# Down projection with 20 of 22 k-tiles in seven products, weight sums from two loads, a GpSimd addition and three adding transfers

## The chip, the cores and the metric

The kernel runs on one core of a Trainium2 chip. The time is that of one execution on the device in microseconds (us). The engines are called as the profile calls them: PE is TensorE, DVE VectorE, ACT ScalarE, POOL GpSimd, and SP issues transfers. The kernel before has a median of 830.14 us over 3 runs (827.84 to 832.91).

## What is computed

One encoder block for 512 tokens of width 1024, in float32:

```python
h = rms_norm(x, norm1_pre)
q, k, v, z, xbc, dt_raw, gates = split_cols(h @ w_in, IN_SPLITS)
attn_out = gqa_attention(q, k, v) @ w_attn_proj       # after RMS norm and axial RoPE
ssd_out = ssd_branch(z, xbc, dt_raw, ...) @ w_ssd_proj
g_attn, g_ssd = split(sigmoid(gates), 2)
x = x + rms_norm((g_attn * attn_out + g_ssd * ssd_out) @ w_out, norm1_post)
h2 = rms_norm(x, norm2_pre)
gate, up = split(h2 @ w_gate_up, 2)                   # 1024 -> 2 x 2816
ffn = (silu(gate) * up) @ w_down                      # 2816 -> 1024
x = x + rms_norm(ffn, norm2_post)
```

## The kernel before

**Split products.** Every float32 product is made of three matmuls on pieces: each operand is cast to fp32r (the high part), the rest is the low part, and lo x hi, hi x lo and hi x hi are summed in PSUM. TensorE does little else than these for the whole kernel; its order is written out by hand, while a scheduler orders the other engines by when it thinks their operands are ready, and all of them work through their queues in order.

**Projection weights.** `weights()` (L103) lists the weights of the front with a letter for how the low part comes about, and `presplit()` (L136) does it. ACT casts the high part in any case (L144). With "v" DVE subtracts, with "g" POOL (L149). With "d" ACT writes the negative of the raw weights (L146), and an accumulating transfer, issued by POOL, loads the weights a second time and adds them (L147). A tile has up to 128x1024 elements; the first kv pieces have 128x864. hT is the transposed normalised input: h by DVE (L294), its high part by ACT (L183), its low part by DVE (L184).

**Down projection.** `act` holds 22 tiles of 128 k-rows x 512 tokens. `down_start()` (L1139) does the first two k-tiles while the last of the FFN still runs; `down()` (L1153) adds four more plainly, each with 24 matmuls of 128x512. The other 16 k-tiles, as pairs from two halves of k, go through a product of 2x2 blocks in seven products in place of eight (48 matmuls each). Its weight sums are formed in the tiles ch and p3 (profile name p): a block is loaded by SP, and others are added by accumulating transfers which POOL issues: `after` (L1225) and `third_weights` (L1281). A weight tile is split by `wsplit` (ACT L1195, DVE L1196), an activation tile by `asplit` into "as" (ACT L1201, DVE L1202). DVE also forms activation sums (L1312 to L1318), with both operands in SBUF, and adds finished banks to the results c (L1245). `begin` and `finish` do the last norm for a token tile t: square sums on ACT, the gain multiplications on DVE (L1257, L1264), then c * r + x (L1270) and the store. They stand between the matmuls of product 7, whose last 24 matmuls are those of the second token tile alone (by_token).

```python
stages.extend((lambda g=g: prep(g), lambda g=g: work(g)) for g in range(NG2))
...
for i, (_, work) in enumerate(stages):
    if i + 1 < len(stages):
        stages[i + 1][0]()
    work()
last(3)
```

The operands of a group are thus recorded one group ahead of its matmuls. The tiles whi and wlo have 4 buffers, "as" has 10; the pool of down() lies where a pool of the FFN was.

Of the kernel before, what the change touches and what calls it, by code (L numbers as in the profile page):

```python
# [14 lines left out]
ALU = mybir.AluOpType  # L15
# [4 lines left out]
P = 128  # L20
# [21 lines left out]
R_DTB, R_AL, R_D, R_QK, R_END = 0, 32, 64, 80, 336  # L42


PAIRS = 8
NPLAIN = 3


# [12 lines left out]
class Block:  # L61
# [41 lines left out]
    def weights(self):  # L103

        a = self.a
        for k0, kn in ((0, 3), (3, 3), (6, 2)):
            yield a["w_kv"][:, k0 : k0 + kn, :], kn * 288, "v" if k0 == 0 else "d"
        for j in range(12):
            yield a["w_xbc"][j], 1024, "g" if j < 3 else "d"
        for n in range(2):  # L110
            for i in range(4):
                yield a["w_z"][n, i], 1024, "gd"[n]
        for j in range(2 * KD):
            yield a["w_g"][j], 1024, "d"
# [1038 lines left out]
    def down(self, pool):  # L1153


        V, A, G, T = self.V, self.A, self.G, self.T
        n0, wd, act = NF - 2 * PAIRS, self.a["w_dn"], self.act
        NG2 = PAIRS // 2
        new = lambda tag, shape, bufs, dt=F32: pool.tile([P] + shape, dt, tag=tag, name=self.nm(tag), bufs=bufs)
        chain = [new("ch", [2, 512], NG2) for _ in range(NG2)]  # L1160
        p3 = [new("p3", [2, 512], NG2) for _ in range(NG2)]
        r1 = [new("r1", [256], PAIRS) for _ in range(PAIRS)]
        splits = [new("as", [2, 256], 10, F32R) for _ in range(10)]
        cs = [new("c", [512], 8) for _ in range(8)]
# [6 lines left out]
        mm3, plain, bank = self.mm3f, self.plain, self.bank  # L1171

        for k in range(1, n0):
            if k > 1:
                self.down_operands(k, pool)
                if k < n0 - 2:
                    for t, n in bank:
                        plain(k, t, n)
            if k == 1:
                gain = [new("gn", [512], 2) for _ in range(2)]  # L1180
                for i in range(2):
                    self.load(gain[i], self.a["norm2_post"][i * 512 : i * 512 + 512].partition_broadcast(P))
            if k >= 2 and k - 2 < NG2:
                self.load(chain[k - 2], blk(k - 2, 0, 0))
        for t, n in reversed(bank):
            for k in (n0 - 2, n0 - 1):
                plain(k, t, n)
# [28 lines left out]
        def product(dst, b, a, start, after=None, sums=None, by_token=None, then=None):  # L1216

            kept = []

            def prep(g):  # L1220
                w = wsplit(b(g))
                for i in range(2):
                    kept.append((asplit(a(2 * g + i)), [y[:, i * 512 : i * 512 + 512] for y in w]))
                if after:
                    G.dma_start(chain[g], after(g), accum_op=ALU.add)  # L1225

            def work(g):
                for k in (2 * g, 2 * g + 1):
                    x, wi = kept[k]
                    for t in range(1 if by_token else 2):  # L1230
                        mm3(dst[t], [y[:, t * P : t * P + P] for y in x], wi, start and k == 0)
                    if sums:
                        sums(k)
                if g == NG2 - 1:
                    if by_token:
                        by_token()
                        for x, wi in kept:
                            mm3(dst[1], [y[:, P : 2 * P] for y in x], wi)
                    if then:
                        then()  # L1240

            stages.extend((lambda g=g: prep(g), lambda g=g: work(g)) for g in range(NG2))

        def add(t, n, p, op=ALU.add):
            V.tensor_tensor(c[t, n], c[t, n], p, op)  # L1245

        half = {}

        def begin(t):

            x = [new("x2", [512], 4) if t < 2 else self.slot("a", [512], name="x2") for _ in range(2)]
# [3 lines left out]
            self.square_sum(ss[:, 0:1], c[t, 1], self.rstd[:, t : t + 1])  # L1255
            V.tensor_scalar(ss[:, 0:1], ss[:, 0:1], 1.0 / D, EPS, ALU.mult, ALU.add)
            V.tensor_tensor(c[t, 1], c[t, 1], gain[1], ALU.mult)  # L1257
            half[t] = x, ss

        def finish(t):  # L1260
            x, ss = half[t]
            r2 = self.rstd[:, t : t + 1]
            self.square_sum(ss[:, 1:2], c[t, 0], r2)
            V.tensor_tensor(c[t, 0], c[t, 0], gain[0], ALU.mult)  # L1264
            v = self.tiny(1, "rv")
            V.tensor_scalar(v, ss[:, 1:2], 1.0 / D, ss[:, 0:1], ALU.mult, ALU.add)
            r = self.rsqrt(v, 1, True)
            V.tensor_tensor(r, r, r2, ALU.mult)
            for i in (1, 0):
                V.scalar_tensor_tensor(c[t, i], c[t, i], r, x[i], ALU.mult, ALU.add)  # L1270
                self.load(self.out[t * P : t * P + P, i * 512 : i * 512 + 512], c[t, i])

        u = [self.ps("sa") for _ in range(2)]
        a = [self.ps("mm") for _ in range(2)]
        x = [self.ps("sb") for _ in range(2)]
        v, y = [bank[t, 0] for t in (0, 1)], [bank[t, 0] for t in (2, 3)]

        def third_weights():
            for g in range(NG2):
                self.load(p3[g], blk(g, 0, 1))  # L1280
                G.dma_start(p3[g], blk(g, 1, 1), accum_op=ALU.add)  # L1281

        def sums2():
            for t in range(2):
# [4 lines left out]
        def second(p):  # L1289
            for t in range(2):  # L1290
                add(2 + t, 1, p[t], ALU.subtract)

        def sums6():
            for t in range(2):
                c[2 + t, 0] = cs.pop()
                A.copy(c[2 + t, 0], u[t])
                add(2 + t, 1, u[t], ALU.subtract)
                add(t, 1, u[t], ALU.subtract)
                add(2 + t, 0, x[t])
                begin(2 + t)  # L1300
# [4 lines left out]

        def last(t):
            add(t, 0, y[t - 2])
            finish(t)

        between = {4: lambda: begin(0), 5: lambda: begin(1), 6: lambda: finish(0), 7: lambda: finish(1)}  # L1310
        product(u, lambda g: chain[g], a11, True, lambda g: blk(g, 0, 1),
                lambda k: V.tensor_tensor(r1[k], a22(k), a21(k), ALU.subtract), then=third_weights)  # L1312
        product(v, lambda g: raw(g, 1, 0), a12, False, None, lambda k: V.tensor_tensor(a21(k), a11(k), a21(k), ALU.subtract),
                then=sums2)
        product(a, lambda g: chain[g], lambda k: r1[k], True, lambda g: blk(g, 1, 1),
                lambda k: V.scalar_tensor_tensor(r1[k], r1[k], -1.0, a11(k), ALU.mult, ALU.subtract), then=lambda: second(a))
# [134 lines left out]
```

## Time and profile before

| what | before |
|---|---|
| median of 3 runs | 830.14 us |
| profiled execution, whole | 830.12 us |
| its span in the trace | 828.2 us |
| PE busy | 804.9 us, 97% |
| DVE busy | 578.4 us, 70% |
| ACT busy | 465.8 us, 56% |
| POOL busy | 200.0 us, 24% |
| share of the chain that ended last | PE 83%, DVE 5%, DMA 4%, ACT 3% |

The span is from the first to the last instruction of the profiled execution; the whole time has about 2 us around it. An engine's busy share says little by itself: where PE waits, and for whom, tells which stage could be shorter. An arrow <- in a row names who released the wait.

### The profile page before, as it was taken

How to read it: one execution, taken by the hardware profiler on the slowest of the kernel's cores; microseconds unless marked ns; L12 is line 12 of the kernel's file. 1: busy time of each engine (PE TensorE's matmuls, PEld its weight loads, DVE VectorE, ACT ScalarE, POOL GpSimd, SP SyncE). 2: the span in 40 equal slices, each digit the busy share in tenths (PEclk: the TensorE clock that was granted, in tenths of full speed). 3: DMA queues.
4: the chain of work that ended last, by engine and by line, in shares of the span. 5: the costliest groups of instructions: out<-in, count | busy, mean ns of one | idle time of the engine just before them, and what ended most of it. 6: DMA issues, size and time to landing. Idle time of an engine off the chain costs nothing.

```text
span 828.2 us, 12209 instructions
## 1 busy us (share of the span) xinstructions
PE 804.9 (97%) x4522; PEld 676.8 (82%) x4522; DVE 578.4 (70%) x999; ACT 465.8 (56%) x841; POOL 200.0 (24%) x162
## 2 busy tenths in 40 slices
PE   8899999999899999999999999999999999999994
PEld 7688887666676777777888798999999999888883
DVE  3959785656335456685783799788888878837988
ACT  7767875745844442166333656555555555536673
POOL 3443430100132244539451002000000100041200
PEclk9999999999999999999999999999999999999998
DMA  9757830620875665137335453667766664899642
GB/s 314 218 134 159 200 93 27 140 64 1 216 176 130 158 150 124 52 114 252 116 129 185 164 153 91 188 193 188 193 177 185 182 178 140 286 288 245 104 93 102
DMA packets 49658, 130.52 MB, mean 158 GB/s; under 512 B 5568, under 2 KB 5952, under 8 KB 49600
## 3 DMA queue, kind: packets, MB, share of 16 engines
q1 hardware_dynamic: 38048, 95.46, 33.7%
q0 software_dynamic: 11552, 34.30, 24.0%
q8 instruction: 35, 0.57, 0.3%
q14 instruction: 23, 0.19, 0.1%
HBM read 121.35 MB, written 8.39 MB: 157 GB/s over the span
## 4 chain that ended last, share of the span: by engine, by line
PE 83%; DVE 5%; DMA 4%; ACT 3%; issue 2%; POOL 1%; SPq 1%; DVEq 0%; ACTq 0%; POOLq 0%
PE sa L972 10%; PE mm L178 8%; PE mm L179 8%; PE mm L180 8%; PE sc L972 7%; PE sb L1125 4%; PE sa L1125 4%; PE mm L972 3%; PE sb L972 3%; PE mm L1125 3%; PE sc L178 3%; PE sc L180 3%; PE sc L179 3%; PE sc L677 2%; PE sa L179 2%
## 5 line engine op out<-in xcount | busy, mean ns | idle before, releaser
L144 ACT CAST whi<-raw 128x1024 fp32r<-128x1024 f32 (+3 forms) x69 | 68.0, 992 | 20.6 <-PE sc L180 9.8
L178 PE MATMUL mm<-hT,wlo 128*128 128x512 f32 x176 | 73.8, 419 | 2.1 <-DMA wlo<-in_w_g 2.1
L149 POOL TENSOR_TENSOR wlo<-raw,whi 128x1024 fp32r<-128x1024 f32 (+1 forms) x28 | 58.2, 2081 | 65.5 <-ACT whi L144 63.9
L180 PE MATMUL mm<-hT,whi 128*128 128x512 f32 x176 | 69.7, 396 | 0.0
L179 PE MATMUL mm<-hT,whi 128*128 128x512 f32 x176 | 69.3, 394 | 0.0
L1023 POOL DMA_DIRECT2D raw<-in_w_gu x19 | 16.4, 861 | 211.5 <-ACT x L1114 54.8
L1028 ACT CAST whi<-raw 128x512 fp32r<-128x512 f32 (+1 forms) x57 | 41.6, 762 | 33.9 <-DMA raw<-in_w_gu 12.9
L1029 DVE TENSOR_TENSOR wlo<-raw,whi 128x512 fp32r<-128x512 f32 (+1 forms) x57 | 47.8, 866 | 16.3 <-ACT whi L1028 16.3
L972 PE MATMUL sa<-R,whi 128*128 128x256 f32 x304 | 56.4, 283 | 0.0
L972 PEld LDWEIGHTS sa<-R,whi 128*128 128x128 f32 x304 | 47.5, 192 | 0.0
L146 ACT ACTIVATE wlo<-raw 128x1024 fp32r<-128x1024 f32 (+2 forms) x31 | 32.3, 1043 | 26.4 <-PE mm L178 24.4
L972 PE MATMUL sa<-R,wlo 128*128 128x256 f32 x152 | 43.1, 283 | 0.0
L178 PEld LDWEIGHTS mm<-hT,wlo 128*128 128x128 f32 x176 | 33.3, 189 | 11.8 <-issue 3.2
L147 POOL DMA_DIRECT2D wlo<-in_w_g x16 | 13.8, 863 | 112.6 <-ACT wlo L146 66.7
L179 PEld LDWEIGHTS mm<-hT,whi 128*128 128x128 f32 x176 | 33.3, 189 | 8.7 <-issue 2.4
L180 PEld LDWEIGHTS mm<-hT,whi 128*128 128x128 f32 x176 | 33.3, 189 | 7.6 <-issue 0.5
L638 DVE TENSOR_REDUCE nmax<-sa 128x1 f32<-128x512 f32 x32 | 21.6, 686 | 19.9 <-PE sa L636 19.7
L972 PE MATMUL sa<-h2T,b 128*128 128x256 f32 x228 | 30.5, 283 | 0.0
L641 ACT ACTIVATE pr<-sa,nmax 128x512 f32<-128x512 f32 x32 | 22.0, 688 | 14.6 <-DVE rc L643 7.4
L972 PEld LDWEIGHTS sa<-R,wlo 128*128 128x128 f32 x152 | 29.2, 192 | 0.0
L155 ACT ACTIVATE junk<-z 128x512 bf16<-128x512 f32 x8 | 5.0, 628 | 42.6 <-DVE z L785 42.5
L972 PEld LDWEIGHTS sa<-h2T,b 128*128 128x128 f32 x228 | 28.7, 192 | 0.0
(475 smaller groups left out, 2552.8 us busy)
## 6 DMA issues: line engine op xcount, KB each, us to landing
raw<-in_w_gu SPq DMA_DIRECT2D x44, 512.0 KB, 4.7
raw<-in_w_gu POOLq DMA_DIRECT2D x19, 512.0 KB, 5.4
raw<-in_w_g SPq DMA_DIRECT2D x16, 512.0 KB, 6.0
wlo<-in_w_g POOLq DMA_DIRECT2D x16, 512.0 KB, 6.8
raw<-in_w_dn SPq DMA_DIRECT2D x14, 512.0 KB, 7.2
raw<-in_w_xbc SPq DMA_DIRECT2D x12, 512.0 KB, 4.9
ch<-in_w_dn POOLq DMA_DIRECT2D x12, 512.0 KB, 7.2
b<-in_w_gu SPq DMA_DIRECT2D x19, 256.0 KB, 5.8
```

The source lines that it names most:

```text
L144: self.A.copy(h[:, :n], raw[:, :n])
L146: self.A.mul(l[:, :n], raw[:, :n], -1.0)
L149: e.tensor_tensor(l[:, :n], raw[:, :n], h[:, :n].bitcast(F32), ALU.subtract)
L178: self.T.matmul(o, ll, rh, start=first, stop=False)
L179: self.T.matmul(o, lh, rl, start=False, stop=False)
L180: self.last_mm = self.T.matmul(o, lh, rh, start=False, stop=last)
L638: V.tensor_reduce(nmax, ps, AX.X, ALU.max, negate=True)
L641: self.last_exp = A.activation(pr, ps, AF.Exp, bias=nmax, accum_out=sm)
L972: self.T.matmul(dst, x, y[:, k], start=start and k == 0 and i == 0, stop=k == 3 and i == 2, skip_group_check=True)
L1028: A.copy(dst[0], src)
L1029: lo.tensor_tensor(dst[1], src, dst[0].bitcast(F32), ALU.subtract)
L1125: self.T.matmul(o, x, y, start=start and i == 0, stop=i == 2, skip_group_check=True)
```

## The change

Five groups of two pairs (20 k-tiles) in place of four go through the seven products, and only two k-tiles stay plain, those of `down_start()`. For each group SP loads two blocks, b11 and ch (the block beside it). After b11 is split for product 1, POOL adds ch to it by a TENSOR_TENSOR of 128x1024 (`first_sums`), and an accumulating transfer adds a third block to ch; product 3 takes the sum in b11, product 4 that in ch, and two more accumulating transfers, after products 4 and 5, change ch for products 5 and 7. That is two loads, a GpSimd addition and three adding transfers where there were two loads and four adding transfers. Six of the eight gain multiplications go to POOL, `begin` and `finish` take the half n of the columns that is ready first, and `finish` of tokens 0 and 1 comes after the last pair (8 and 9) of product 7. In the front seven low parts go from "d" to "v": the second kv piece, four tiles of z, two of the gates.

```diff
-PAIRS = 8
+PAIRS = 10
-            yield a["w_kv"][:, k0 : k0 + kn, :], kn * 288, "v" if k0 == 0 else "d"
+            yield a["w_kv"][:, k0 : k0 + kn, :], kn * 288, "d" if k0 == 6 else "v"
-                yield a["w_z"][n, i], 1024, "gd"[n]
+                yield a["w_z"][n, i], 1024, "gv"[n]
-            yield a["w_g"][j], 1024, "d"
+            yield a["w_g"][j], 1024, "v" if j < 2 else "d"
...
-        p3 = [new("p3", [2, 512], NG2) for _ in range(NG2)]
+        b11 = [new("b11", [2, 512], NG2) for _ in range(NG2)]
...
-        for k in range(1, n0):
-            if k > 1:
-                self.down_operands(k, pool)
...
-            if k >= 2 and k - 2 < NG2:
-                self.load(chain[k - 2], blk(k - 2, 0, 0))
-        for t, n in reversed(bank):
-            for k in (n0 - 2, n0 - 1):
-                plain(k, t, n)
+        for g in range(NG2):
+            self.load(b11[g], blk(g, 0, 0))
+            self.load(chain[g], blk(g, 0, 1))
...
-                    G.dma_start(chain[g], after(g), accum_op=ALU.add)
+                    after(g)
...
-                    for t in range(1 if by_token else 2):
+                    for t in range(1 if by_token and g >= NG2 - 4 else 2):
...
-                        for x, wi in kept:
+                        for x, wi in kept[2 * (NG2 - 4) :]:
...
-        def begin(t):
+        def begin(t, n):
...
-            V.tensor_tensor(c[t, 1], c[t, 1], gain[1], ALU.mult)
+            G.tensor_tensor(c[t, n], c[t, n], gain[n], ALU.mult)
...
-            V.tensor_tensor(c[t, 0], c[t, 0], gain[0], ALU.mult)
+            (G if t < 2 else V).tensor_tensor(c[t, n], c[t, n], gain[n], ALU.mult)
...
-        def third_weights():
-            for g in range(NG2):
-                self.load(p3[g], blk(g, 0, 1))
-                G.dma_start(p3[g], blk(g, 1, 1), accum_op=ALU.add)
+        def more(k, n):
+            return lambda g: G.dma_start(chain[g], blk(g, k, n), accum_op=ALU.add)
+        def first_sums(g):
+            G.tensor_tensor(b11[g], b11[g], chain[g], ALU.add)
+            more(1, 1)(g)
...
+        def third():
+            second(x)
+            for t in range(2):
+                begin(t, 0)
...
-        between = {4: lambda: begin(0), 5: lambda: begin(1), 6: lambda: finish(0), 7: lambda: finish(1)}
-        product(u, lambda g: chain[g], a11, True, lambda g: blk(g, 0, 1),
+        between = {8: lambda: finish(0, 1), 9: lambda: finish(1, 1)}
+        product(u, lambda g: b11[g], a11, True, first_sums,
...
-        product(a, lambda g: chain[g], lambda k: r1[k], True, lambda g: blk(g, 1, 1),
+        product(a, lambda g: b11[g], lambda k: r1[k], True, None,
...
-        product(x, lambda g: p3[g], a21, True, None,
+        product(x, lambda g: chain[g], a21, True, more(0, 0),
...
-        product(u, lambda g: chain[g], lambda k: r1[k], False, lambda g: blk(g, 1, 0), then=sums6)
+        product(u, lambda g: chain[g], lambda k: r1[k], False, more(1, 0), then=sums6)
```

The order of DVE after the change in product 1, from the last sums in front of the first weight tile to the second one (wlo is a low part of weights, as of activations, r a sum of activations):

```order
L1311 TENSOR_TENSOR r_1527_7375<-act_4342,act_5464 128x256
L1187 TENSOR_TENSOR wlo_7423<-b_1517_7365,whi_7422 128x1024
L1193 TENSOR_TENSOR as_7388<-act_5866,as_7388 128x256
L1193 TENSOR_TENSOR as_7389<-act_6000,as_7389 128x256
L1311 TENSOR_TENSOR r_1528_7376<-act_4343,act_5598 128x256
L1311 TENSOR_TENSOR r_1529_7377<-act_4344,act_5732 128x256
L1311 TENSOR_TENSOR r_1530_7378<-act_4345,act_5866 128x256
L1311 TENSOR_TENSOR r_1531_7379<-act_4346,act_6000 128x256
L1187 TENSOR_TENSOR wlo_7433<-b_1518_7366,whi_7432 128x1024
```

Before, the weight tiles of product 1 stood one behind the other, since all the small operations were ahead of them; now six small operations stand between the first and the second tile. Between the next ones stand 7, 5 and 3.

POOL before, in the down projection (p and ch are sums of weight blocks):

```order
L1281 DMA p_1522_7383<-in_w_dn 128x2x512
L1281 DMA p_1523_7384<-in_w_dn 128x2x512
L1225 DMA ch_7379<-in_w_dn 128x2x512
L1281 DMA p_1524_7385<-in_w_dn 128x2x512
L1281 DMA p_1525_7386<-in_w_dn 128x2x512
L1225 DMA ch_7380<-in_w_dn 128x2x512
```

POOL after the change, at the same place (b is b11):

```order
L1274 TENSOR_TENSOR b_1517_7365<-b_1517_7365,ch_7360 128x1024
L1271 DMA ch_7360<-in_w_dn 128x2x512
L1274 TENSOR_TENSOR b_1518_7366<-b_1518_7366,ch_7361 128x1024
L1271 DMA ch_7361<-in_w_dn 128x2x512
L1274 TENSOR_TENSOR b_1519_7367<-b_1519_7367,ch_7362 128x1024
L1271 DMA ch_7362<-in_w_dn 128x2x512
```

POOL now adds tiles of 128x1024 itself, in turn with the transfers; each addition waits for the low part (wlo) of its tile on DVE.

DVE around the z tiles after the change (nmax are the row maxima of a softmax):

```order
L149 TENSOR_TENSOR wlo_1691<-raw_1688,whi_1690 128x1024
L655 COPY pt_1595<-sb_1590 128x512
L149 TENSOR_TENSOR wlo_1697<-raw_1694,whi_1696 128x1024
L149 TENSOR_TENSOR wlo_1703<-raw_1700,whi_1702 128x1024
L184 TENSOR_TENSOR aTl_1627<-sc_1617,aTh_1626 128x512
L638 TENSOR_REDUCE nmax_1647<-sa_1644 128x1
L638 TENSOR_REDUCE nmax_1658<-sa_1655 128x1
L149 TENSOR_TENSOR wlo_1709<-raw_1706,whi_1708 128x1024
```

The four L149 rows are new on DVE; the other rows stood there before in the same order.

## Rows read from the trace of the kernel before

**Rows 1.** The page: busy us of each engine, share of the span, instructions.
```profile
PE 804.9 (97%) x4522; PEld 676.8 (82%) x4522; DVE 578.4 (70%) x999; ACT 465.8 (56%) x841; POOL 200.0 (24%) x162
```

**Rows 2.** TensorE's waits: us in all, times, the longest.
```profile
PE sb L179 <- DMA wlo<-in_w_kv: 3.3, 1, 3.3
PE mm L178 <- DMA wlo<-in_w_g: 2.1, 1, 2.1
PE mm L179 <- DMA wlo<-in_w_z: 1.8, 2, 1.3
```

**Rows 3.** Windows: busy us by engine (instructions), then granted clock, DMA share, GB/s.
```profile
38.70:42.70 4.00, 4.00 (x19) 4.00 (x20) 1.63 (x3) 4.00 (x8) 0.36 (x1) 0.57 0.57 208
213.10:216.50 3.40, 3.40 (x9) 2.65 (x10) 0.62 (x2) 1.04 (x1) 0.00 (x0) 0.53 1.06 273
150.00:200.00 50.00, 48.17 (x239) 32.83 (x240) 30.28 (x76) 29.84 (x63) 3.42 (x4) 1.00 0.36 85
```

**Rows 4.** Chain that ended last: start, us, what; two in kv, one at the gates.
```profile
39.06 0.13 PE sb L180
...
39.52 0.24 PE sb L180
...
213.71 0.43 PE mm L179
```

**Rows 5.** Timeline at 33.6 (GpSimd), then lines of VectorE: duration ns min/median/max.
```profile
33.58 2.38 POOL L149 TENSOR_TENSOR wlo<-raw,whi 128x1024 fp32r<-128x1024 f32 x1 [1.82 <-ACT whi L144]
...
L294 DVE SCALAR_TENSOR_TENSOR h<-xT,gcol,rbs x8: 739/742/2884, 26.3 to 37.1; 128x512 f32<-128x512 f32 x8
...
L862 DVE TENSOR_TENSOR gs<-gs,at x8: 676/2545/2904, 402.3 to 433.4; 128x512 f32<-128x512 f32 x8
...
L861 DVE TENSOR_TENSOR gs<-gs,mm x4: 672/680/682, 401.1 to 428.0; 128x512 f32<-128x512 f32 x4
```

**Rows 6.** VectorE, down projection: one timeline row, a group by line, the chain.
```profile
710.34 0.69 DVE L1055 SCALAR_TENSOR_TENSOR act<-up,g 128x512 f32<-128x512 f32 x1
...
L1196 DVE TENSOR_TENSOR wlo<-ch,whi 128x1024 fp32r<-128x1024 f32 x16 | 19.5, 1224 | 13.2 <-ACT whi L1195 13.1
...
808.39 0.67 DVE as L1202 x2
```

**Rows 7.** Chain at the start of down; TensorE at products 1 and 7.
```profile
706.62 1.39 PE sc L1125 x6
708.01 1.43 PE sa L972 x12
...
740.59 0.39 PE L1125 MATMUL sa<-whi,as 128*128 128x512 f32 x1
...
805.87 0.39 PE L1125 MATMUL sc<-whi,as 128*128 128x512 f32 x1
```

**Rows 8.** Timeline of TensorE in product 7.
```profile
807.68 0.62 PE L1125 MATMUL sc<-whi,as 128*128 128x512 f32 x2
...
808.36 0.98 PE L1125 MATMUL sc<-whi,as 128*128 128x512 f32 x2
...
810.10 0.39 PE L1125 MATMUL sc<-whi,as 128*128 128x512 f32 x1
810.68 0.47 PE L1125 MATMUL sc<-whi,as 128*128 128x512 f32 x1 [0.20 <-DVE as L1202]
```

**Rows 9.** Timeline of SP's queue; DMA issues: KB each, median us to landing.
```profile
709.76 0.90 SPq L101 DMA_DIRECT2D gn<-in_norm_post  x2
...
ch<-in_w_dn SPq DMA_DIRECT2D x4, 512.0 KB, 8.0
```

**Rows 10.** Timeline of the tail: TensorE's last, then VectorE.
```profile
817.34 0.39 PE L1125 MATMUL sc<-whi,as 128*128 128x512 f32 x1
...
818.62 0.68 DVE L1245 TENSOR_TENSOR c<-c,sc 128x512 f32<-128x512 f32 x1
...
821.50 0.69 DVE L1264 TENSOR_TENSOR c<-c,gn 128x512 f32<-128x512 f32 x1
```

More of the change, by code (lines that the diff above doesn't have):

```diff
@@ L1169, in blk @@
             return wd[j : j + 2, :, n * 512 : n * 512 + 512].rearrange("k p c -> p k c")
-        mm3, plain, bank = self.mm3f, self.plain, self.bank
-        for k in range(1, n0):
-            if k > 1:
-                self.down_operands(k, pool)
-                if k < n0 - 2:
-                    for t, n in bank:
-                        plain(k, t, n)
[L1179 to L1182, printed above, removed]
-            if k >= 2 and k - 2 < NG2:
-                self.load(chain[k - 2], blk(k - 2, 0, 0))
-        for t, n in reversed(bank):
-            for k in (n0 - 2, n0 - 1):
-                plain(k, t, n)
+        mm3, bank = self.mm3f, self.bank
+        for g in range(NG2):
+            self.load(b11[g], blk(g, 0, 0))
+            self.load(chain[g], blk(g, 0, 1))
+        gain = [new("gn", [512], 2) for _ in range(2)]
+        for i in range(2):
+            self.load(gain[i], self.a["norm2_post"][i * 512 : i * 512 + 512].partition_broadcast(P))
         c = {(t, 1): cs.pop() for t in (2, 3, 0, 1)}
@@ L1254, in begin, with finish @@
             ss = self.tiny(2, "ss")
-            self.square_sum(ss[:, 0:1], c[t, 1], self.rstd[:, t : t + 1])
+            self.square_sum(ss[:, 0:1], c[t, n], self.rstd[:, t : t + 1])
             V.tensor_scalar(ss[:, 0:1], ss[:, 0:1], 1.0 / D, EPS, ALU.mult, ALU.add)
-            V.tensor_tensor(c[t, 1], c[t, 1], gain[1], ALU.mult)
+            G.tensor_tensor(c[t, n], c[t, n], gain[n], ALU.mult)
             half[t] = x, ss
-        def finish(t):
+        def finish(t, n):
             x, ss = half[t]
             r2 = self.rstd[:, t : t + 1]
-            self.square_sum(ss[:, 1:2], c[t, 0], r2)
-            V.tensor_tensor(c[t, 0], c[t, 0], gain[0], ALU.mult)
+            self.square_sum(ss[:, 1:2], c[t, n], r2)
+            (G if t < 2 else V).tensor_tensor(c[t, n], c[t, n], gain[n], ALU.mult)
             v = self.tiny(1, "rv")
@@ L1268, in finish @@
             V.tensor_tensor(r, r, r2, ALU.mult)
-            for i in (1, 0):
+            for i in (1 - n, n):
                 V.scalar_tensor_tensor(c[t, i], c[t, i], r, x[i], ALU.mult, ALU.add)
@@ L1299, in sums6 @@
                 add(2 + t, 0, x[t])
-                begin(2 + t)
+                begin(2 + t, 1)
         def sums3():
@@ L1307, in last @@
             add(t, 0, y[t - 2])
-            finish(t)
-        between = {4: lambda: begin(0), 5: lambda: begin(1), 6: lambda: finish(0), 7: lambda: finish(1)}
-        product(u, lambda g: chain[g], a11, True, lambda g: blk(g, 0, 1),
-                lambda k: V.tensor_tensor(r1[k], a22(k), a21(k), ALU.subtract), then=third_weights)
+            finish(t, 0)
+        between = {8: lambda: finish(0, 1), 9: lambda: finish(1, 1)}
+        product(u, lambda g: b11[g], a11, True, first_sums,
+                lambda k: V.tensor_tensor(r1[k], a22(k), a21(k), ALU.subtract))
         product(v, lambda g: raw(g, 1, 0), a12, False, None, lambda k: V.tensor_tensor(a21(k), a11(k), a21(k), ALU.subtract),
                 then=sums2)
-        product(a, lambda g: chain[g], lambda k: r1[k], True, lambda g: blk(g, 1, 1),
+        product(a, lambda g: b11[g], lambda k: r1[k], True, None,
                 lambda k: V.scalar_tensor_tensor(r1[k], r1[k], -1.0, a11(k), ALU.mult, ALU.subtract), then=lambda: second(a))
-        product(x, lambda g: p3[g], a21, True, None,
-                lambda k: V.scalar_tensor_tensor(a12(k), r1[k], -1.0, a12(k), ALU.mult, ALU.subtract), then=lambda: second(x))
-        product(u, lambda g: chain[g], lambda k: r1[k], False, lambda g: blk(g, 1, 0), then=sums6)
+        product(x, lambda g: chain[g], a21, True, more(0, 0),
+                lambda k: V.scalar_tensor_tensor(a12(k), r1[k], -1.0, a12(k), ALU.mult, ALU.subtract), then=third)
+        product(u, lambda g: chain[g], lambda k: r1[k], False, more(1, 0), then=sums6)
         product(a, lambda g: raw(g, 1, 1), a12, False, then=sums3)
```

## The prediction

> **What bounds the kernel now.** I read the page first: TensorE is busy for 804.9 of 828.2 us, VectorE for 578.4 [rows 1]. So time can be won in two ways only: fewer matmuls, or shorter waits of TensorE. The list of TensorE's waits names the three that this change aims at, all for low parts that come through an accumulating transfer: 3.3 us at the kv weights, 2.1 at the first gate weights, 1.8 at z [rows 2]. Behind the first and the third the clock is low: the granted clock is 0.57 in 38.7 to 42.7 and 0.53 in 213.1 to 216.5, the 1.2 GHz level, against 1.00 in 150 to 200 [rows 3]; one kv matmul takes 0.24 us there instead of 0.13, one gate matmul 0.43 [rows 4]. Before both stretches TensorE had stood idle for 3.3 and 2.1 us. The sum is made against the profiled execution (828.2 us of span, 830.12 with what lies around it), which stands at the median of the runs, 830.14.
>
> **The front.** Seven low parts go from a ScalarE multiplication and an accumulating transfer to a VectorE subtraction. kv: the wait of 3.3 goes and the low clock with it. The stretch of 0.24 us steps from 39.52 to 42.7 holds some 13 matmuls, so 13 x 0.11 = 1.4 us. What is late next is the low part of hT: VectorE's products for it stand behind one more subtraction (1 us), and one of them already takes 2.9 us instead of 0.74 [rows 5]. I leave 0.7 us for that: gain 3.3 + 1.4 - 0.7 = 4.0. z: 1.5 of the 1.8 (four tiles; the rest is the first). Gates: 2.1 and 8 matmuls x (0.43 - 0.23, the usual step, below) = 1.6, together 3.7. The seven subtractions are new work for VectorE, up to 1.22 us each [rows 6], and around z it is busy for 30.28 of 50 us [rows 3]; the two of the gates stand straight ahead of softmax reductions. Between nothing and 6 x 1.2 = 7.3 us, I take 1.0, since TensorE has projection matmuls to do beside the softmax. Later gate tiles keep the transfer and will be wanted 3.7 us earlier; that is in the 1.0 too. **Front: -8.2 us** (bounds -10 and -1).
>
> **Fewer matmuls.** Before, 144 plain matmuls and 336 in products; after, 48 and 420: 12 fewer. Six products of 48 matmuls run from 740.59 to 805.87 [rows 7], so one costs 65.28 / 288 = 0.227 us: **-2.7 us**. Product 7 has two stalls where the splits of VectorE come late: a pair of matmuls takes 0.98 us instead of 0.62, and one waits at 810.68, 0.58 after the one before instead of 0.23 [rows 8]: the gain multiplications that stood there go to GpSimd: **-0.7 us**.
>
> **Product 1.** This is where I expect the gain to be given back. In the order of VectorE after the change, wlo of b11_0 stands behind 14 small operations and the wlo of b11_1 to b11_4 follow with 6, 7, 5 and 3 small operations between. Each wlo releases one GpSimd addition of 128x1024. A GpSimd subtraction of that size took 2.38 us at 33.58, and beside it one L294 operation of VectorE took 2.9 us instead of 0.74; the same at L862, where the median of eight is 2.5 us against 0.68, while L861 beside it, which reads one operand from PSUM, keeps to 0.68 [rows 5]. So a VectorE operation with both operands in SBUF stands still while GpSimd adds. The Trainium skill states this as a rule ("SBUF — State Buffer", section "Who interferes with whom"): such a VectorE instruction and a GpSimd instruction that reads SBUF exclude each other, and the loser waits for the whole instruction. By that rule, with which the rows here agree, the addition is no free help from an idle engine.
>
> From the end of wlo b11_0 to the end of wlo b11_4 VectorE then needs 21 small operations x 0.335 us (two as take 0.67) = 7.0, four wlo x 1.14 = 4.6, and four holds of 2.14 (2.88 - 0.74, as at L294), 8.6: together 20.2 us. (1.14 is the 1.22 less the overlap with the next.) TensorE needs 4 x 12 x 0.227 = 10.9 for the same groups.
>
> When does it start? SP issues the first load of the new pool at 709.8 [rows 9], where the order now has b11_0; the four ch loads of before landed after a median of 8.0 us [rows 9]; they shared the transfer engines, and for the first of the queue I take 6.5. So b11_0 is there at 716.3, its cast (1.05 us) done at 717.3, wlo at 718.5. VectorE itself would be there at 711.0 (end of the last act, 710.34 + 0.69 [rows 6]) + 14 x 0.335 + 1.14 = 716.8, so the load decides. TensorE wants b11_0 at 706.62 + 1.43 (the 12 FFN matmuls between, [rows 7]) + 48 x 0.227 = 718.9: 0.4 us to spare. **Stall: 20.2 - 10.9 - 0.4 = +8.9 us**, in four pieces of about 2.2. Bounds: 0, if the additions hold nothing up, and 12 with the landing at 8.0 and a hold of the addition's full 2.38. After pieces of that length the clock fell above, so some matmuls run at 0.43: 7 of them are **+1.5 us**; this hardly adds up, since a group of twelve at 0.43 takes 5.2 us, about what VectorE needs for one anyway.
>
> **Products 2 to 7.** Two gain multiplications of 128x512 on GpSimd after product 4 hold VectorE for about half of 2.14 each, and the queue of VectorE is full there already; the first loads for product 2 stand before b11 on SP and are early. VectorE has 3 wlo, 14 as and 8 sums more in all, and comes out of product 1 late. I take **+1.7 us** (0 to 4). The accumulating transfers of product 1 queue on GpSimd behind the additions, but their sums are read in product 4 only, over 20 us later: nothing.
>
> **Tail.** The last bank is done at 817.34 + 0.39, its addition starts only at 818.62 and its gain multiplication at 821.50, since the four and two L1270 of other tokens stand ahead [rows 10]. After the change the finishing of tokens 0 and 1 stands ahead of the last addition but their gains are GpSimd's. Of the 1.0 late start and the 1.0 or so between I take **-1.8 us** (0 to -2.5).
>
> **Sum.** -8.2 - 2.7 - 0.7 + 8.9 + 1.5 + 1.7 - 1.8 = -1.3, so 830.1 - 1.3 = **828.8 us**. A measurement here tells about 0.5% (4.15 us) from no change.
>
> **Rivals.**
> A, the additions are hidden: GpSimd gets its turns in gaps of VectorE. For it: VectorE's operations here are 0.3 us long, so GpSimd might get its turns between them without holding one up for its whole length. Against it: the rows of L294 and L862. Product 1 then needs 11.6 us where TensorE needs 10.9, so a stall of 0.3, no low clock, nothing in products 2 to 7: -8.2 - 2.7 - 0.7 + 0.3 - 1.8 = -13.1, **817.0 us**. Chance 0.20.
>
> B, slower: the seven subtractions stand in VectorE's queue in front of the softmax and of hT, and TensorE waits for each: 7 x 1.22 = 8.5 us of the 9.2 that the front gives. It decides from the point where TensorE's own matmuls no longer cover a subtraction, that is where the reductions behind it come later than the last projection matmul issued beside them. Front -0.7, the down projection +6.9 (the sum above without the front): +6.2, **836.3 us**. For it: the two gate subtractions stand immediately in front of two reductions; against it: VectorE is free for 40% of the time around z [rows 3]. Chance 0.12.
>
> C, the clock: the stalls keep TensorE at the lower level through all 60 matmuls of product 1, 60 x 0.43 = 25.8 us instead of 13.6: +12.2 in place of 8.9 + 1.5. For it: a wait of 2.1 was followed by 0.53 [rows 3]; against it: the waits are shorter at half clock. **830.6 us**, chance 0.10.
>
> **Numbers.** The forecast has 0.58. Its own range, from the bounds of the front and of product 1, is 822 to 835; a quarter of it lies below 826.0, 0.15 above 834.3. Faster by over 0.5%: 0.20 + 0.58 x 0.25 = 0.35, and 0.01 of C: 0.36. Slower: 0.58 x 0.15 + 0.12 + 0.02 = 0.23. The rest, 0.41, is within 0.5%. The range takes in A and B but for their outer halves: 816.5 to 836.3.
>
> **What would show it.** Right: the three waits of rows 2 gone and the granted clock near 1.00 there; in product 1 four TensorE waits of about 2 us for wlo or as of VectorE, with single VectorE operations of 2 to 3 us beside the additions of L1274. Wrong: no such waits (A), or reductions of L638 that start later after a wlo (B). If TensorE waits in product 1 for transfers, the loads were mis-sized, not the holds.

## The result, and the profile after

The change made the kernel slower: 838.92 us (median of 5 runs, 837.87 to 840.77) against 832.64 us (median of 5 runs). The ratio on record is 1.0101 with a 95% interval of 1.0076 to 1.0126; it is not the quotient of the two medians, which is 1.0075. The forecast was 828.8 us with a range up to 836.3. The span of the profiled execution grew by 10.4 us, from 828.2 to 838.6; that is more than the medians show, since the profiled execution after the change is the slowest of its five (840.77 us) and the one before is at 830.12. The account below is of these two executions.

The page after, in the columns of [rows 1]: TensorE is busy for as long as before although it has twelve matmuls fewer; VectorE is busy for 30 us more and GpSimd for 37.

```profile
PE 805.5 (96%) x4510; PEld 674.6 (80%) x4510; DVE 608.9 (73%) x1021; ACT 462.5 (55%) x847; POOL 236.7 (28%) x165
```

**The front.** TensorE's waits after, in the columns of [rows 2]:

```profile
PE sa L1125 <- DVE wlo L1187: 8.1, 2, 7.3
PE sa L1125 <- ACT whi L1186: 3.0, 1, 3.0
PE mm L1125 <- DVE ss L1247: 2.7, 1, 2.7
PE sa L268 <- DVE ones L264: 1.1, 1, 1.1
PE sc L178 <- ACT whi L274: 0.9, 1, 0.9
PE sb L178 <- DVE hT L184: 0.9, 1, 0.9
```

None of the three waits of [rows 2] is left; the last row, 0.9 us for hT, is what came next at kv. The windows confirm it, in the columns of [rows 3]: TensorE is busy for 50.00 of 50 us around z with a granted clock of 1.00, although VectorE does 32.29 us of work there now in place of 30.28.

```profile
20.00:50.00 30.00, 28.99 (x163) 24.82 (x162) 27.20 (x40) 21.34 (x40) 13.71 (x9) 1.00 0.53 166
150.00:200.00 50.00, 50.00 (x250) 33.85 (x249) 32.29 (x68) 24.49 (x55) 0.00 (x0) 1.00 0.13 43
200.00:250.00 50.00, 49.91 (x218) 35.06 (x217) 21.90 (x38) 30.88 (x47) 10.71 (x11) 1.00 0.69 168
...
720.00:730.00 10.00, 4.52 (x13) 3.28 (x13) 10.00 (x8) 0.42 (x2) 8.78 (x6) 0.66 0.83 138
...
760.00:770.00 10.00, 10.00 (x46) 8.29 (x45) 10.00 (x20) 5.68 (x12) 10.00 (x2) 1.00 0.01 2
770.00:780.00 10.00, 6.27 (x27) 4.51 (x25) 4.82 (x10) 1.66 (x3) 7.96 (x6) 0.99 0.67 114
800.00:810.00 10.00, 6.49 (x22) 4.78 (x21) 5.19 (x8) 6.99 (x14) 2.58 (x2) 0.86 0.33 93
```

The chain reaches the down projection at 697.04 us where it was there at 706.62 [rows 7]. So what lies ahead of it gave 9.6 us; e4 below has the front alone.

```profile
697.04 1.39 PE sc L1125 x6
```

**The down projection.** From here all is lost again, and 10 us more. A product begins where its bank's first matmul starts in TensorE's timeline; so each is worked out from the difference of two starts (product 7: to the start of its last matmul), and a wait for the first operand of a product counts with the product before it. With 60 matmuls of 0.227 us a product needs 13.6 us, and 13.4 for the last one so measured.

| product | 1 | 2 | 3 | 4 | 5 | 6 | 7 |
|---|---|---|---|---|---|---|---|
| after | 23.4 | 15.7 | 13.6 | 16.9 | 16.2 | 19.2 | 13.6 |
| lost | 9.8 | 2.1 | 0 | 3.3 | 2.6 | 5.6 | 0.2 |

The losses are 23.6 us. Twelve matmuls fewer give back 2.7, and the 0.8 us that product 7 lost before (817.34 - 805.87 - 47 x 0.227) are gone; with the front that is 23.6 - 2.7 - 0.8 - 9.6 = +10.5, against 10.4 in the spans.

Where do they come from? In the windows above, the granted clock is below 1.00 and TensorE idle in 720 to 730, in 770 to 780 (the clock follows just behind) and in 800 to 810. The timeline of GpSimd, with the start, the duration, and in brackets the idle time before:

```profile
707.41 9.09 POOL L1274 TENSOR_TENSOR b<-b,ch 128x1024 f32<-128x1024 f32 x1 [33.14 <-DVE wlo L1187]
...
717.58 2.81 POOL L1274 TENSOR_TENSOR b<-b,ch 128x1024 f32<-128x1024 f32 x1
...
721.47 2.79 POOL L1274 TENSOR_TENSOR b<-b,ch 128x1024 f32<-128x1024 f32 x1
...
755.32 16.53 POOL L1248 TENSOR_TENSOR c<-c,gn 128x512 f32<-128x512 f32 x2 [20.49 <-ACT junk L155]
771.79 6.17 POOL L1271 DMA_DIRECT2D ch<-in_w_dn  x5
```

The first addition of 128x1024 takes 9.09 us, the next two 2.8; the two gain multiplications of 128x512 take 16.53 us together, where GpSimd took 2.38 for a tile of twice that size [rows 5]. In 750 to 770 VectorE is busy without a gap, and GpSimd finishes one of the two, at 768.18. Only then, at 771.79, can it issue the five adding transfers which are queued behind. VectorE in product 1:

```profile
713.83 2.96 DVE L1193 TENSOR_TENSOR as<-act,as 128x256 fp32r<-128x256 f32 x2
716.71 4.31 DVE L1312 TENSOR_TENSOR act<-act 128x256 f32<-128x256 f32 x3
720.94 4.41 DVE L1187 TENSOR_TENSOR wlo<-b,whi 128x1024 fp32r<-128x1024 f32 x1
725.28 3.18 DVE L1193 TENSOR_TENSOR as<-act,as 128x256 fp32r<-128x256 f32 x2
```

When GpSimd does get its turn, VectorE stands: two splits of 0.42 us take 2.96, three sums 4.31, and one wlo of 1.22 takes 4.41. So the exclusion works in both directions.

The rows also show where a starved GpSimd gets its turn. The first addition ends at 716.50; 2.38 us back from there [rows 5] is 714.1, where VectorE's second split had to wait for its cast by ACT (713.85 to 714.26). The first multiplication ends 1.2 us after VectorE has come to two additions which read one operand from PSUM:

```profile
755.32 12.86 POOL L1248 TENSOR_TENSOR c<-c,gn 128x512 f32<-128x512 f32 x1 [20.49 <-ACT junk L155]
...
766.94 1.28 DVE L1236 TENSOR_TENSOR c<-c,mm 128x512 f32<-128x512 f32 x2
```

From 755.32 to 766.94 all of VectorE's operations read two operands in SBUF, one behind the other. So GpSimd waits here until VectorE has a gap or an operation of another kind, and not for a single operation. Why the additions from 717.58 on got their turn at once is not shown.

TensorE pays for both directions, in product 1 and at the start of product 5:

```profile
725.41 0.80 PE L1125 MATMUL sa<-wlo,as 128*128 128x512 f32 x1 [7.29 <-DVE wlo L1187]
...
778.80 0.49 PE L1125 MATMUL sa<-whi,as 128*128 128x512 f32 x1 [3.03 <-ACT whi L1186]
```

ACT shows the second payment and a third one: the cast of ch for product 5 waits 11 us for the transfer that GpSimd issued late, and a cast in product 6 waits 7.2 us for a load. The 2.1 us of product 2 are a cast's wait for a load too (5.27 us, at 743.37).

```profile
777.70 1.04 ACT L1186 CAST whi<-ch 128x1024 fp32r<-128x1024 f32 x1 [11.06 <-DMA ch<-in_w_dn]
...
803.01 1.04 ACT L1186 CAST whi<-raw 128x1024 fp32r<-128x1024 f32 x1 [7.21 <-DMA raw<-in_w_dn]
```

**The tail.** From the start of TensorE's last matmul to the end of the span it is 838.6 - 827.75 = 10.9 us, as before (828.2 - 817.34). GpSimd's two multiplications take 5.14 us,

```profile
817.19 5.14 POOL L1255 TENSOR_TENSOR c<-c,gn 128x512 f32<-128x512 f32 x2 [8.76 <-ACT junk L155]
```

to 822.33, and VectorE's own small operations for tokens 0 and 1 last to 822.61. The four large ones of these tokens follow at 822.64, then the whole finishing of token 2, so the last addition starts at 830.24, 2.1 us after the last bank is done (0.9 in [rows 10]). Its gain multiplication follows 1.6 us behind it, where it was 2.9.

```profile
822.64 2.74 DVE L1261 SCALAR_TENSOR_TENSOR c<-c,ry,x 128x512 f32<-128x512 f32 x4
825.29 0.68 DVE L1236 TENSOR_TENSOR c<-c,sc 128x512 f32<-128x512 f32 x1
...
828.90 1.41 DVE L1261 SCALAR_TENSOR_TENSOR c<-c,ry,x 128x512 f32<-128x512 f32 x2
830.24 0.68 DVE L1236 TENSOR_TENSOR c<-c,sc 128x512 f32<-128x512 f32 x1
```

### The profile page after: what moved, and what is told of

Read it like the earlier page. It is cut to its first block, busy times and chain, and to the rows that moved or that the text cites. A ratio compares the mean times of both kernels' runs of the same rounds, so it can differ in the third digit from the quotient of the medians.

```text
span 838.6 us, 12230 instructions
## 1 busy us (share of the span) xinstructions
PE 805.5 (96%) x4510; PEld 674.6 (80%) x4510; DVE 608.9 (73%) x1021; ACT 462.5 (55%) x847; POOL 236.7 (28%) x165
## 4 chain that ended last, share of the span: by engine, by line
PE 75%; DVE 10%; DMA 6%; issue 4%; ACT 4%; POOL 1%; DVEq 0%; SPq 0%; ACTq 0%; POOLq 0%
PE sa L972 10%; PE mm L178 8%; PE mm L179 8%; PE mm L180 8%; PE sc L972 7%; PE mm L972 3%; PE sb L972 3%; DVE wlo L1187 3%; PE sc L178 3%; PE sc L180 3%; PE sc L179 3%; DMA raw<-in_w_dn 2%; PE sc L677 2%; PE sb L653 2%; DMA ch<-in_w_dn 2%
## 5 line engine op out<-in xcount | busy, mean ns | idle before, releaser
L149 POOL TENSOR_TENSOR wlo<-raw,whi 128x1024 fp32r<-128x1024 f32 (+1 forms) x28 | 58.5, 2093 | 65.2 <-ACT whi L144 63.8
L1023 POOL DMA_DIRECT2D raw<-in_w_gu x19 | 16.3, 859 | 212.5 <-DMA raw<-in_w_gu 69.6
L144 ACT CAST whi<-raw 128x1024 fp32r<-128x1024 f32 (+3 forms) x65 | 63.9, 989 | 19.5 <-PE sc L180 12.5
L1029 DVE TENSOR_TENSOR wlo<-raw,whi 128x512 fp32r<-128x512 f32 (+1 forms) x57 | 49.4, 893 | 16.5 <-ACT whi L1028 16.3
L147 POOL DMA_DIRECT2D wlo<-in_w_g x14 | 12.1, 862 | 145.1 <-PE mm L179 81.1
L146 ACT ACTIVATE wlo<-raw 128x1024 fp32r<-128x1024 f32 (+1 forms) x24 | 25.1, 1047 | 24.4 <-PE mm L178 24.4
L1274 POOL TENSOR_TENSOR b<-b,ch 128x1024 f32<-128x1024 f32 x5 | 20.7, 4142 | 33.5 <-DVE wlo L1187 33.5
L1125 PE MATMUL sa<-whi,as 128*128 128x512 f32 x80 | 27.2, 417 | 3.0 <-ACT whi L1186 3.0
L766 DVE COPY_PREDICATED sa<-cst,sa 128x512 f32<-128x512 uint32 x16 | 11.1, 693 | 24.7 <-PE sa L763 24.7
```

The costliest lines, as they stand in the source:

```text
L144: self.A.copy(h[:, :n], raw[:, :n])
L146: self.A.mul(l[:, :n], raw[:, :n], -1.0)
L149: e.tensor_tensor(l[:, :n], raw[:, :n], h[:, :n].bitcast(F32), ALU.subtract)
L1029: lo.tensor_tensor(dst[1], src, dst[0].bitcast(F32), ALU.subtract)
L1125: self.T.matmul(o, x, y, start=start and i == 0, stop=i == 2, skip_group_check=True)
```

## The experiments

All kernels were timed beside the kernel before on the same chip. The table has the ratio to it and the us of each product as above. Runs e1 to e4, e5 to e8, e9 and e10, and e11 and e12 were timed together; across these groups the ratio is the better measure. The kernels of e5, e8 and e10 leave sums out or overwrite them, so their times price a part and are no versions of the kernel.

| run | us | ratio (95%) | 1 | 2 | 3 | 4 | 5 | 6 |
|---|---|---|---|---|---|---|---|---|
| the change | 838.9 | 1.0101 (1.0076 to 1.0126) | 23.4 | 15.7 | 13.6 | 16.9 | 16.2 | 19.2 |
| e1_gain_dve | 829.9 | 1.0000 (0.9987 to 1.0012) | 24.0 | 13.6 | 13.6 | 13.6 | 13.6 | 15.1 |
| e2_add_dma | 843.7 | 1.0174 (1.0151 to 1.0198) | 20.2 | 21.5 | 13.6 | 16.3 | 16.1 | 19.2 |
| e3_both | 834.2 | 1.0057 (1.0039 to 1.0076) | 22.1 | 20.9 | 13.6 | 13.6 | 13.6 | 17.5 |
| e4_front | 819.8 | 0.9881 (0.9857 to 0.9904) | | | | | | |
| e5_no_add | 823.3 | 0.9944 (0.9925 to 0.9964) | 20.2 | 13.6 | 13.6 | 13.6 | 13.6 | 14.1 |
| e6_add_dve | 826.4 | 0.9973 (0.9953 to 0.9993) | 13.9 | 19.5 | 13.6 | 13.6 | 14.1 | 16.8 |
| e7_add_dve_late | 822.5 | 0.9930 (0.9911 to 0.9949) | 14.0 | 13.6 | 14.1 | 13.6 | 14.2 | 18.2 |
| e8_memset | 823.4 | 0.9943 (0.9923 to 0.9964) | 20.3 | 13.8 | 13.6 | 13.6 | 13.6 | 15.0 |
| e9_early_loads | 818.4 | 0.9869 (0.9848 to 0.9891) | 14.0 | 13.6 | 13.8 | 13.6 | 14.2 | 13.6 |
| e10_no_add_no_transfer | 815.1 | 0.9832 (0.9805 to 0.9859) | 13.9 | 13.6 | 13.6 | 13.6 | 13.6 | 13.6 |
| e11_gain_pool | 826.7 | 0.9972 (0.9954 to 0.9990) | 14.0 | 13.8 | 14.4 | 20.9 | 16.2 | 13.6 |
| e12_front_beside | 819.6 | 0.9893 (0.9864 to 0.9921) | | | | | | |

**e1: the gain multiplications back on VectorE.**

```diff
-            G.tensor_tensor(c[t, n], c[t, n], gain[n], ALU.mult)
+            V.tensor_tensor(c[t, n], c[t, n], gain[n], ALU.mult)
...
-            (G if t < 2 else V).tensor_tensor(c[t, n], c[t, n], gain[n], ALU.mult)
+            V.tensor_tensor(c[t, n], c[t, n], gain[n], ALU.mult)
```

> The changed kernel with its six GpSimd gain multiplications back on VectorE; the GpSimd additions of product 1 stay. Theory P (GpSimd and VectorE exclude each other while both read SBUF, in both directions: two gain multiplications that take 16.5 us on GpSimd hold back the adding transfers queued behind them, and products 4 to 6 lose 11.4 us by that): product 5 no longer waits 3.0 us for whi, products 4 to 6 take about 41 us in place of 52.2, product 1 stays at about 23.4 us; time about 828 us. Theory T (too many transfers at once, landing late): no transfer is changed, so the time stays within 2 us of 838.9.

Products 4 to 6 fall from 52.3 to 42.3 us and the time by 9.0 us, with no transfer changed: theory P is right here and theory T wrong. In the change the multiplications start only at 755.32, in product 3, so the 2.1 us of product 2, which are gone as well, cannot be theirs: the load that was waited for there landed sooner in this execution. TensorE's timeline keeps the wait of product 1 and a small one in product 6:

```profile
726.18 0.80 PE L1125 MATMUL sa<-wlo,as 128*128 128x512 f32 x1 [7.30 <-DVE wlo L1187]
...
798.08 0.50 PE L1125 MATMUL mm<-wlo,as 128*128 128x512 f32 x1 [1.16 <-DVE wlo L1187]
```

**e2 and e3: the addition by an accumulating transfer**, with the gains on GpSimd (e2) and on VectorE (e3).

```diff
-            G.tensor_tensor(b11[g], b11[g], chain[g], ALU.add)
+            G.dma_start(b11[g], blk(g, 0, 1), accum_op=ALU.add)
```

> The changed kernel with the GpSimd addition of b11 and ch replaced by an accumulating transfer of the same block; the gain multiplications stay on GpSimd. Theory P: product 1 falls from 23.4 us to about 14, product 2 from 15.7 to about 13.6, products 4 to 6 stay at about 52 us; time about 827 us. Theory T: five more transfers of 512 KB, so product 1 does not gain and the later products lose up to 4 us; 837 to 843 us.

> Both at once: no elementwise work on GpSimd in the down projection. Theory P: products 1 to 7 take about 13.6 us each; 838.9 - 9.8 - 2.1 - 11.4 = 815.6, with the six gains on VectorE again about 817 us. Theory T: 835 us or more.

Both theories miss e2: product 1 gains 3.2 us, product 2 loses 5.8, and 843.7 us lies above either. Theory P misses e3: without any elementwise work of GpSimd, product 1 of e3 still takes 22.1 us and product 2 loses 7.3. Here theory T has its place, and the 834.2 us are close to what it said. ACT's casts in e3 wait for the loads of the last two blocks,

```profile
715.53 1.05 ACT L1186 CAST whi<-b 128x1024 fp32r<-128x1024 f32 x1 [1.80 <-DMA b<-in_w_dn]
...
723.60 1.04 ACT L1186 CAST whi<-b 128x1024 fp32r<-128x1024 f32 x1 [6.40 <-DMA b<-in_w_dn]
```

while the transfer engines are busy all the time (the column behind the clock):

```profile
710.00:720.00 10.00, 9.69 (x43) 7.69 (x42) 7.41 (x17) 4.35 (x9) 3.58 (x3) 1.00 1.10 262
720.00:730.00 10.00, 5.43 (x15) 3.63 (x14) 5.33 (x7) 5.21 (x8) 3.72 (x4) 0.74 1.11 261
```

The load of b11_4 was issued at 702.45 and its cast starts at 723.60. The five transfers that replace the additions are dearer here than the additions: e3 is 4.3 us slower than e1.

**e4 and e12: the front alone**, in the kernel before.

```diff
-            yield a["w_kv"][:, k0 : k0 + kn, :], kn * 288, "v" if k0 == 0 else "d"
+            yield a["w_kv"][:, k0 : k0 + kn, :], kn * 288, "d" if k0 == 6 else "v"
-                yield a["w_z"][n, i], 1024, "gd"[n]
+                yield a["w_z"][n, i], 1024, "gv"[n]
-            yield a["w_g"][j], 1024, "d"
+            yield a["w_g"][j], 1024, "v" if j < 2 else "d"
```

> The kernel before with the seven low parts of the front changed from accumulating transfers to VectorE subtractions, nothing else. In the traces the down projection starts 9.6 us earlier after the change. If that is all the front's doing and holds by itself: 832.6 - 9.6 = 823 us. Rival: part of it is the FFN's doing or is lost again later: 826 us or more.

The gain is 9.6 us (819.8 against 829.4 for the kernel before in these runs), and it lasts to the end; e12, the same kernel in another group, has a ratio of 0.9893. The longest waits of TensorE that are left are small, and none is for a low part that a transfer brings:

```profile
PE sa L268 <- DVE ones L264: 1.1, 1, 1.1
PE mm L178 <- ACT at L693: 1.0, 2, 0.6
PE sc L178 <- ACT whi L274: 0.9, 1, 0.9
```

**e5 and e10: without the addition, and without the transfer behind it.**

```diff
         def first_sums(g):
-            G.tensor_tensor(b11[g], b11[g], chain[g], ALU.add)
-            more(1, 1)(g)
```

(e5 leaves out the first of these lines, e10 both.)

> As e1_gain_dve (gains on VectorE), and the addition of ch to b11 is left out, so product 3 works without that block. Every load, adding transfer and VectorE operation stays. Theory P (the GpSimd addition holds VectorE up): product 1 falls from 24.0 us to about 14, time about 820 us. Theory L (ten loads of 512 KB come at once and land late, with or without the addition): product 1 stays above 20 us, time 827 us or more.

> As e5_no_add, and the adding transfer that follows the addition (B22 into ch) is left out too, so products 3 and 4 work with wrong sums. In e5 product 1 took 20.2 us, its wait being for the cast of the last block, whose load landed late. If early adding transfers crowd the loads out: without them product 1 takes about 13.9 us, time about 817 us. Rival: the ten loads alone are late: product 1 stays above 18 us, time above 821 us.

e5 gives only 3.8 of the 10.4 us back: product 1 is as theory L had it, and the time, 823.3 us, lies between the two. Product 1 does not wait for VectorE any more but for the cast of the last block: in ACT's timeline of e5 its load lands late,

```profile
714.79 1.05 ACT L1186 CAST whi<-b 128x1024 fp32r<-128x1024 f32 x1 [0.49 <-DMA b<-in_w_dn]
...
722.86 1.04 ACT L1186 CAST whi<-b 128x1024 fp32r<-128x1024 f32 x1 [5.83 <-DMA b<-in_w_dn]
```

and in e10, where the adding transfers are gone too, the cast follows at once and nothing is lost in any product:

```profile
715.05 1.05 ACT L1186 CAST whi<-b 128x1024 fp32r<-128x1024 f32 x1
...
717.77 1.05 ACT L1186 CAST whi<-b 128x1024 fp32r<-128x1024 f32 x1
```

So product 1 has two walls, one behind the other. Behind the starved addition the first adding transfer was issued at 716.79, late enough to let the loads through; in e5 it is issued at 706.57, and the transfers crowd the last load out.

**e6 and e7: the addition on VectorE**, at its place (e6) and asked for by product 2 (e7).

```diff
-            G.tensor_tensor(b11[g], b11[g], chain[g], ALU.add)
+            V.tensor_tensor(b11[g], b11[g], chain[g], ALU.add)
...
-        product(u, lambda g: b11[g], a11, True, first_sums,
+        product(u, lambda g: b11[g], a11, True, None,
-        product(v, lambda g: raw(g, 1, 0), a12, False, None, ...
+        product(v, lambda g: raw(g, 1, 0), a12, False, first_sums, ...
```

(The last four lines are e7's.)

> As e1_gain_dve, with the five additions on VectorE. Theory P: nothing excludes anything now; VectorE has 11.6 + 4 x 1.14 = 16.2 us of work from wlo b11_0 to wlo b11_4 where TensorE needs 10.9, with about 2 us to spare: product 1 takes about 17 us, time about 823 us, that is faster than with the addition on the otherwise idle GpSimd. Theory L: product 1 stays above 20 us.

> As e6_add_dve, with the additions asked for one product later, which puts two of the five behind the last weight tile of product 1 on VectorE. Theory P: product 1 takes about 15.5 us, time about 821.5 us. Rival: VectorE is full in products 2 and 3 as well, so what is moved is lost there: 823 us or more.

Five more operations of 1.2 us on the engine that was held up, and product 1 takes 13.9 us: it loses 0.3 where the GpSimd addition costs 10. In e6 the loss goes on to product 2 (5.9 us), and the time, 826.4 us, misses what was expected. A load of product 2 now lands late, behind the adding transfers:

```profile
731.95 1.04 ACT L1186 CAST whi<-raw 128x1024 fp32r<-128x1024 f32 x1 [7.61 <-DMA raw<-in_w_dn]
```

In e7 two of the additions, and with them two of the adding transfers, come later (726.74 and 735.12 in place of 717.78 and 721.87), and products 1 to 5 lose 1.5 us in all; the time, 822.5 us, lies between theory P and the rival. What stays is product 6. In ACT's timeline, a cast waits for a load, and the square sum of the norm stands behind that cast, so VectorE waits for both:

```profile
784.81 1.05 ACT L1186 CAST whi<-raw 128x1024 fp32r<-128x1024 f32 x1 [4.65 <-DMA raw<-in_w_dn]
785.77 0.72 ACT L155 ACTIVATE junk<-c,rstd 128x512 bf16<-128x512 f32 x1
```

**e8: a GpSimd operation that only writes.**

```diff
-            G.tensor_tensor(b11[g], b11[g], chain[g], ALU.add)
+            G.memset(b11[g], 0.0)
```

> As e1_gain_dve, with a GpSimd memset of b11 in the place of the GpSimd addition (product 3 then works on zeros): it waits for the same wlo, stands at the same place of the queue, and only writes. Theory P, by which the common reading of SBUF is the cause: VectorE is not held up, single VectorE operations stay below 1.3 us, product 1 takes about 14 us as without the addition, time about 820 us. Rival O (that GpSimd works on SBUF at all, or that its queue is late, is enough): product 1 stays above 20 us, time above 827 us.

The memset stands at the addition's place, takes 0.95 to 1.45 us, and VectorE beside it keeps its durations (four sums at 711.14: 1.42 us; two splits at 714.62: 0.88, against 0.89 in e10, where GpSimd does nothing there). GpSimd:

```profile
711.28 0.95 POOL L1274 MEMSET b<- 128x1024 f32 x1 [0.60 <-DVE wlo L1187]
...
714.81 0.96 POOL L1274 MEMSET b<- 128x1024 f32 x1 [1.43 <-issue]
```

VectorE:

```profile
711.14 1.42 DVE L1312 TENSOR_TENSOR act<-act 128x256 f32<-128x256 f32 x4
...
714.62 0.88 DVE L1193 TENSOR_TENSOR as<-act,as 128x256 fp32r<-128x256 f32 x2
```

Product 1 still takes 20.3 us, as in e5, so the number that was expected is missed; but it is e5's wait for the last load (2.9 us at 724.25), not VectorE's. As for the holds, the operation that reads nothing makes none here.

**e9: the weights of product 6 loaded early.**

```diff
-        product(a, lambda g: b11[g], lambda k: r1[k], True, None,
+        product(a, lambda g: b11[g], lambda k: r1[k], True, lambda g: self.load(b11[g], blk(g, 1, 1)),
...
-        product(a, lambda g: raw(g, 1, 1), a12, False, then=sums3)
+        product(a, lambda g: b11[g], a12, False, then=sums3)
```

> As e7_add_dve_late, with the weights of product 6 loaded into the tiles of b11, which are free after product 3, in place of the three buffers of raw, of which the last two loads come free only during product 6. If product 6's 18.2 us are that wait for a buffer: product 6 takes about 13.8 us, time about 818 us, ahead of the front alone (819.8). Rival: VectorE or the adding transfers set product 6 anyway: 821 us or more.

Product 6 takes 13.6 us, and the kernel 818.4: faster than both kernels of the study. Whether it is faster than the front alone can't be told: 0.9869 (0.9848 to 0.9891) here, 0.9893 (0.9864 to 0.9921) for the latter where it was timed again (e12).

> The front alone once more (the same kernel as e4_front), on the chip and beside the runs of e11_gain_pool, to set a version with the repaired down projection (e9_early_loads, 0.9869 of before) against it: 12 matmuls of 0.227 us fewer are 2.7 us. If the repaired rearrangement pays: this one lies at 0.989 of before or above, 820 us. Rival: it pays nothing: 0.987 or below.

**e11: e9 with the gain multiplications on GpSimd again.**

```diff
-            V.tensor_tensor(c[t, n], c[t, n], gain[n], ALU.mult)
+            G.tensor_tensor(c[t, n], c[t, n], gain[n], ALU.mult)
...
-            V.tensor_tensor(c[t, n], c[t, n], gain[n], ALU.mult)
+            (G if t < 2 else V).tensor_tensor(c[t, n], c[t, n], gain[n], ALU.mult)
```

> As e9_early_loads (818.4 us), with the six gain multiplications on GpSimd again, as the change has them: two of them stand ahead of ten adding transfers in GpSimd's queue. Theory P: VectorE's unbroken queue keeps GpSimd from its operands for over 10 us, the transfers for product 5 start late, product 5 waits: 5 to 11 us more, 823 to 829 us. Rival: the 16.5 us were only a consequence of product 1's delay, and without that the multiplications find gaps: within 2 us of 818.4.

8.3 us more, and 0.9972 against 0.9869 as ratios. GpSimd needs 20.69 us for two multiplications, and the transfers follow:

```profile
742.70 20.69 POOL L1248 TENSOR_TENSOR c<-c,gn 128x512 f32<-128x512 f32 x2 [6.80 <-ACT junk L155]
763.34 6.16 POOL L1271 DMA_DIRECT2D ch<-in_w_dn  x5
```

TensorE waits 7.1 us at the start of product 5:

```profile
772.01 0.76 PE L1125 MATMUL sa<-whi,as 128*128 128x512 f32 x1 [7.12 <-DVE as L1193]
```

So the starvation does not come from a delay in product 1. The turns come as in the change: the first multiplication ends at 755.91, beside two additions that read PSUM,

```profile
742.70 13.21 POOL L1248 TENSOR_TENSOR c<-c,gn 128x512 f32<-128x512 f32 x1 [6.80 <-ACT junk L155]
...
754.66 1.29 DVE L1236 TENSOR_TENSOR c<-c,mm 128x512 f32<-128x512 f32 x2
```

and the second at 763.39, 1.1 us after VectorE has run out of work (762.25). Two operations of about 1.3 us each, moved off VectorE to relieve it, cost the kernel most of 8 us. A kernel with the multiplications behind the transfers in GpSimd's queue was not run.

## Why the prediction was wrong

**Wrong: the term for products 2 to 7.** It was put at +1.7 us (0 to 4): "Two gain multiplications of 128x512 on GpSimd after product 4 hold VectorE for about half of 2.14 each", while the adding transfers of product 1 were put at "nothing" and those behind the multiplications, for product 5, had no term. Products 2 to 6 lost 13.6 us; e1 brings back 10.0 of these in products 4 to 6. Measured in the two spans the sum missed by 11.8 us (-1.3 forecast, +10.5 found), and this term alone by 11.9. The prediction took the rows of L294 and L862 [rows 5] as the whole of the matter: GpSimd runs for its 2.4 us and VectorE waits. The rule of the Trainium skill that it named ("SBUF — State Buffer", section "Who interferes with whom") has it both ways: whoever issues first has the ports for the whole instruction, and the other blocks. The trace agrees that either can be the one that waits, but not as to the length: against a queue of VectorE without a gap GpSimd waits for many instructions, so that the first addition takes 9.09 us and two multiplications 16.53. What is late then are the transfers in GpSimd's queue, which stand behind the multiplications in the order that was at hand. That the ch of product 5 depends on them could have been read from that order, and e1 and e11 show that moving the multiplications was worth 9.0 and 8.3 us.

**Product 1: the size right, the reason half right.** +8.9 and 1.5 for the clock were forecast, 9.8 measured, most of it a wait of 7.3 and 1.8 for the 24 matmuls at a low clock behind it. VectorE's stretch from wlo b11_0 to wlo b11_4 was as foreseen, 22.7 us (707.27 to 729.93) against 20.2. But TensorE did not wait four times for 2.2 us but once for 7.29, since the first addition was starved and the holds came together. And the wait for loads, which the forecast named only as a way of being wrong, stood behind it: e5 loses 6.6 us to it without any addition, and e10 nothing without the adding transfers that stand between. That the total came out right is in part luck, since the forecast had only one of the two walls. I put the late loads down to the four plain k-tiles that are gone, which gave TensorE 96 x 0.227 = 21.8 us of work while loads and adding transfers landed; no run brought them back beside the new sums, so this much is argued.

**Right: the front.** -8.2 forecast, -9.6 measured, alone (e4) and in the change. The 1.0 set aside for the new subtractions was not needed. With that rival B has its sign right, slower, and its mechanism wrong.

**Right: the matmuls** (-2.7; e10, in which no product loses, has products of 13.6 us) **and product 7** (-0.7 forecast, -0.6 measured).

**Wrong: the tail.** -1.8 forecast, 0 measured. The gap between the last addition and its gain multiplication shrank by 1.3 us, but the addition itself starts 1.2 us later behind the last bank than before, since the finishing of token 2 now stands whole in front of it. That GpSimd's multiplications (5.14 us) are the cause is not shown: from the last matmul's start to the end it is 9.7 us in e11, which has them on GpSimd, and 10.1 in e9, which has them on VectorE.

**The rivals.** A (additions hidden) fell in the trace of the change. C's clock is seen in 720 to 730 (0.66), though not through the whole product: it is back at 1.00 in 730 to 740.

## What to carry to other kernels

An idle GpSimd is no free help to a VectorE that works on two SBUF operands without a gap: either may hold up the other, GpSimd may get its turn only at VectorE's next gap or PSUM operand, and its own queue, with every transfer that it issues, waits along. Before such an operation is moved there, look at what stands behind it in GpSimd's queue, and try VectorE itself first; here product 1 with the additions on VectorE lost 0.3 us. Work that is taken from TensorE may have been the cover under which the next stage's loads landed, so ask what has to be there now at its start, and behind which transfers it queues.

## What the runs showed of the hardware beyond what was expected

GpSimd can be kept from its operands for very long: 20.69 us for two multiplications of 128x512, while in the same run one at 790.79, beside three additions of VectorE that read one operand from PSUM (L1236), takes 1.29 us. In its long waits GpSimd got its turn where VectorE came to an operation with fewer than two operands in SBUF or had nothing ready (714.1, 766.94 and 770.61 after the change, 754.66 and 762.25 in e11), and not between two operations with both operands in SBUF. A GpSimd memset of 128x1024 in the place of the additions lengthened no VectorE operation by over 0.2 us. And five adding transfers of 512 KB in place of the five GpSimd additions were the dearer here, where the transfer engines were already full (a share of 1.10 in 710 to 720 of e3; e2 against the change 4.8 us, e3 against e1 4.3).
